# A weight load of 128 partitions cut into 32 and 96 at the head of a streamed bilinear kernel

## The chip, the cores and the metric

The kernel runs on one core of a Trainium2 chip. The metric is the device time of one execution in microseconds, the median of several runs. The profile's span is a little shorter than that time: it runs from the first to the last instruction that the profiler records.

## What is computed

```python
def setup_inputs():
    batch, dim_i, dim_j, dim_k = 32, 256, 256, 128
    # x [32, 256], y [32, 256], weight [128, 256, 256], all float32

def reference(x, y, weight):
    return np.einsum('bi,bj,kij->bk', x, y, weight).astype(np.float32)
```

For each of the 128 values of k there is a matrix of 256 x 256, and the output is x W_k y for every row of the batch. The weights are 128 x 256 x 256 x 4 B = 33.6 MB, and each is used once per row of the batch, so the kernel is in the main a stream of the weights from memory.

## The kernel before

The 128 matrices are handled as 32 groups of four. A group lies on chip as 128 partitions: partition p belongs to matrix p mod 4 of the four (`KK = 4`) and to row block p // 4 of the matrix (`IP = 32` blocks of `IC = 8` rows). Each partition has 8 x 256 = 2,048 elements of the group, one contiguous run of 8,192 bytes in memory. This view of the weights is made here:

```python
    def rows_of(groups):
        step = G // len(groups)
        v = weight.rearrange("(u s) (ip ic) j -> s ip u (ic j)", s=step, ic=IC)
        return v[groups[0]]
```

For one group it has the shape 32 x 4 x 2,048: the slowest dimension in memory is the row block, of size 32.

Thirty of the groups are loaded by GpSimd's software queue in eleven transfers (`LOADS`), which cast float32 to bfloat16 on the way into `w_sb`. They are large at first and small at the end, so that little work is left when the last one lands. Two groups, `FIRST = (0, 16)`, go another way: they are loaded as float32 into a buffer `w_f` by the hardware queues of SyncE and ScalarE, and ScalarE casts them into `w_sb`.

```python
LOADS = (
    ((8, 24), 0, 8),
    ((4, 12, 20, 28), 0, 8),
    (tuple(range(2, 32, 4)), 0, 8),
    (tuple(range(1, 32, 4)), 0, 8),
    # ... smaller and smaller
    ((31,), 7, 8),
)
FIRST = (0, 16)

    sw = [
        nc.gpsimd.dma_start(
            out=w_of(groups)[:, :, lo * J:hi * J],
            in_=rows_of(groups)[:, :, lo * J:hi * J],
        ).then_inc(s, 16).ins
        for (groups, lo, hi), s in zip(LOADS, s_w)
    ]
    # the load of y is put behind the second of them

    hw = [
        nc.scalar.dma_start(out=x_sb, in_=x).then_inc(s_x, 16).ins,
    ]
    for n, (g, queue) in enumerate(zip(FIRST, (nc.sync, nc.scalar))):
        hw.append(
            queue.dma_start(
                out=w_f[:, n:n + 1, :], in_=rows_of((g,)),
            ).then_inc(s_f[n], 16).ins
        )
```

All these issues are moved to the very head of the program, ahead of its opening instructions. The cast of the two first groups on ScalarE:

```python
    for n, g in enumerate(FIRST):
        for h in range(2):
            lo, hi = h * IC * J // 2, (h + 1) * IC * J // 2
            c = act.copy(out=w_sb[:, place_of[g], lo:hi], in_=w_f[:, n, lo:hi])
            if h == 0:
                c._wait_ge(s_f[n], 16)
            c.then_inc(s_act, 1)
```

VectorE meanwhile builds `xblk`, x arranged as stationary matrices, and `y4`, y repeated over the partitions. TensorE then works through units of 16, 8, 4, 2, 1 and 1 groups (`UNITS`), each matmul waiting for the load that brings its weights; VectorE multiplies the sums by `y4` and adds them up into `acc`, which SyncE stores.

```python
    pe.wait_ge(s_act, 2 * len(FIRST))
    pe.wait_ge(s_dve, t_x)
    # for each unit: 8 steps of matmuls, each waiting for its load
            c = product(
                ps[:, bank + h, :n, :],
                xblk[:, ic, :, :].rearrange("p b kk -> p (b kk)"),
                w_sb[:, p0 + o:p0 + o + n, ic * J:(ic + 1) * J],
                # ...
            )
            if need:
                c._wait_ge(need[-1], 16)
    # then on VectorE: tmp = ps * y4, acc = sum of tmp over j

    sp.dma_start(out=out_v, in_=acc)._wait_ge(s_dve, n_dve).then_inc(s_out, 16)
```

Of the kernel before, what the change touches and what calls it, by code (L numbers as in the profile page):

```python
# [29 lines left out]
)  # L30

FIRST = (0, 16)
BANKS = 8


@with_exitstack
def kernel(
# [7 lines left out]
    nc = tc.nc  # L45
# [10 lines left out]
    KK = P // B  # L56
# [9 lines left out]
    def sbuf(name, shape, dtype):  # L66
        return nc.alloc_sbuf_tensor(name, shape, dtype).ap()

    def rows_of(groups):


        step = G // len(groups)
        assert all(g == groups[0] + n * step for n, g in enumerate(groups))
        v = weight.rearrange("(u s) (ip ic) j -> s ip u (ic j)", s=step, ic=IC)
        return v[groups[0]]

    def w_of(groups):
        at = [place_of[g] for g in groups]
        step = at[1] - at[0] if len(at) > 1 else 1
        assert all(a == at[0] + n * step for n, a in enumerate(at))  # L80
        return w_sb[:, at[0]:at[-1] + 1:step, :]

    w_sb = sbuf("w_sb", [P, G, IC * J], bf16)
    w_f = sbuf("w_f", [P, len(FIRST), IC * J], f32)
    x_sb = sbuf("x_sb", [B, I], f32)
# [10 lines left out]
    acc = sbuf("acc", [P, G], f32)  # L96
    ps = nc.alloc_psum_tensor("ps", [P, BANKS, 2, J], f32).ap()

# [4 lines left out]
        for s, (groups, lo, hi) in zip(s_w, LOADS) for g in groups for ic in range(lo, hi)  # L103
    }
    s_f = [nc.alloc_semaphore(f"f{g}") for g in FIRST]
    s_x = nc.alloc_semaphore("x")
# [14 lines left out]
            out=w_of(groups)[:, :, lo * J:hi * J],  # L121
            in_=rows_of(groups)[:, :, lo * J:hi * J],
# [6 lines left out]
    hw = [  # L129
        nc.scalar.dma_start(out=x_sb, in_=x).then_inc(s_x, 16).ins,  # L130
    ]
    for n, (g, queue) in enumerate(zip(FIRST, (nc.sync, nc.scalar))):
        hw.append(
            queue.dma_start(
                out=w_f[:, n:n + 1, :], in_=rows_of((g,)),
            ).then_inc(s_f[n], 16).ins
        )
    for ins in [*hw, *sw]:
        tc.no_tile_sem_insts.add(ins.name)

# [8 lines left out]
    for blk in blocks:  # L149
# [20 lines left out]
        out=ident, in_=ident, compare_op=mybir.AluOpType.not_equal, fill=1.0,  # L170
# [3 lines left out]

    for n, g in enumerate(FIRST):
        for h in range(2):
            lo, hi = h * IC * J // 2, (h + 1) * IC * J // 2
            c = act.copy(out=w_sb[:, place_of[g], lo:hi], in_=w_f[:, n, lo:hi])  # L178
            if h == 0:
                c._wait_ge(s_f[n], 16)  # L180
            c.then_inc(s_act, 1)


# [2 lines left out]
    def done(ins):  # L186
# [6 lines left out]
        out=x_rep,  # L193
        in_=x_sb.rearrange("b (ip ic) -> b ic ip", ic=IC).unsqueeze(3)
        .to_broadcast([B, IC, IP, KK]),
    )._wait_ge(s_x, 16))
    for q in range(Q):
        c = v.transpose(  # L198
            out=xt[q * 32:(q + 1) * 32, :, :],
            in_=x_rep[:, :, q * IP // Q:(q + 1) * IP // Q, :],  # L200
        )
# [4 lines left out]
        out=mask, in_=ident.rearrange("p (ip kk) -> p kk ip", kk=KK), axis=AX, op=add,  # L206
    )._wait_ge(s_pool, 2))

    for kk in range(KK):
        c = v.tensor_scalar(  # L210
            out=xblk[:, :, :, kk], in0=xt, scalar1=mask[:, kk:kk + 1],
            scalar2=None, op0=mult,
        )
# [6 lines left out]
        out=yt, in_=y_sb.rearrange("b (jb j) -> b jb j", j=32),  # L220
    )._wait_ge(s_y, 16))
    t = done(v.tensor_copy(  # L222
        out=y_rep, in_=yt.unsqueeze(3).to_broadcast([B, J // 32, B, KK]),
    )._wait_ge(s_dve, t))
    BQ = B // Q
    for q in range(Q):
        c = v.transpose(  # L227
            out=y4[q * 32:(q + 1) * 32, :].rearrange("p (jb j) -> p jb j", j=32),
            in_=y_rep[:, :, q * BQ:(q + 1) * BQ, :],
        )  # L230
# [5 lines left out]
    def product(out, lhsT, rhs, first, last, load):  # L236
        return pe.add_instruction(mybir.InstMatmult(  # L237
            name=nc.get_next_instruction_name(), engine=mybir.EngineType.PE,
            ins=[pe.lower_ap(rhs), pe.lower_ap(lhsT)], outs=[pe.lower_ap(out)],
            start_tensor_calc=first, stop_tensor_calc=last,  # L240
            tile_size=(P, P), tile_position=(0, 0), ldweights=load,
        ))

    pe.wait_ge(s_act, 2 * len(FIRST))
    pe.wait_ge(s_dve, t_x)
    at_dve = t_x
    n_pe = 0
    freed = [0] * BANKS
    landed = set()
    p0 = bank = 0  # L250
    held = None
    for u, unit in enumerate(UNITS):

        n_g = len(unit)
        n_b = (n_g + 1) // 2
        if bank + n_b > BANKS:
            bank = 0
# [8 lines left out]
        for n_step, (ic, h) in enumerate(steps):  # L266
            n = n_g // n_b
# [7 lines left out]
            for s in need[:-1]:  # L275
                pe.wait_ge(s, 16)
# [4 lines that stand above are left out]
                first=(ic == order[0]), last=(ic == order[-1]), load=(held != ic),  # L281
            )
# [10 lines left out]
        if n_g > 1:  # L293
            t = done(v.tensor_tensor(  # L294
                out=prod, in0=sums, in1=y4.unsqueeze(1).to_broadcast([P, n_g, J]), op=mult,
# [3 lines left out]
                out=acc[:, unit[0]:unit[-1] + 1:unit[1] - unit[0]], in_=prod, axis=AX, op=add,  # L299
            )._wait_ge(s_dve, t))  # L300
        else:
            done(v.tensor_tensor_reduce(  # L302
                out=prod[:, 0, :], in0=sums[:, 0, :], in1=y4, scale=1.0, scalar=0.0,
# [44 lines left out]
```

## Time and profile before

| what | value |
|---|---|
| time, median of 3 runs | 84.98 us (84.9 to 85.03) |
| span of the profiled execution | 83.4 us |
| TensorE busy | 32.5 us (39%) |
| VectorE busy | 25.2 us (30%) |
| ScalarE busy | 5.2 us (6%) |
| GpSimd busy | 8.8 us (11%) |
| read from memory | 33.62 MB, 403 GB/s over the span |
| first float32 group (SyncE's queue), issue to landing | 4.9 us |
| second float32 group (ScalarE's queue), issue to landing | 8.3 us |

The profile is of one execution. Its page has the busy time of each engine, the span in 40 equal slices (a digit is the busy share in tenths; DMA is the mean over the core's 16 DMA engines), the DMA queues with packets, megabytes and the time of their packets, the chain of work that ended last, groups of instructions by line, and the DMA issues. Other views of the same trace list who waited for whom (total, times, longest), the chain piece by piece (start, length, what), instructions in order of time (start, length, what) and the busy time of each engine in chosen stages. PE is TensorE, PEld its weight load, DVE VectorE, ACT ScalarE, POOL GpSimd, SP SyncE; L134 is line 134 of the kernel. An engine's name with a q behind it (SPq) is the sequencer that issues.

### The profile page before, as it was taken

How to read it: one execution, taken by the hardware profiler on the slowest of the kernel's cores; microseconds unless marked ns; L12 is line 12 of the kernel's file. 1: busy time of each engine (PE TensorE's matmuls, PEld its weight loads, DVE VectorE, ACT ScalarE, POOL GpSimd, SP SyncE). 2: the span in 40 equal slices, each digit the busy share in tenths (PEclk: the TensorE clock that was granted, in tenths of full speed). 3: DMA queues.
4: the chain of work that ended last, by engine and by line, in shares of the span. 5: the costliest groups of instructions: out<-in, count | busy, mean ns of one | idle time of the engine just before them, and what ended most of it. 6: DMA issues, size and time to landing. Idle time of an engine off the chain costs nothing.

```text
span 83.4 us, 257 instructions
## 1 busy us (share of the span) xinstructions
PE 32.5 (39%) x136; PEld 4.3 (5%) x43; DVE 25.2 (30%) x28; ACT 5.2 (6%) x5; POOL 8.8 (11%) x18
## 2 busy tenths in 40 slices
PE   0000000000000000000099999996029999884780
PEld 0000000000000000000000000000000110112330
DVE  0009450000292000000000000003999800999932
ACT  0019930000000000000000000000000000000000
POOL 5999600000000000000000000000000000000000
PEclk9999999999999999999999999999995799999998
DMA  4999999999999999999999999999999999999980
GB/s 122 393 370 293 214 214 212 216 218 212 218 218 216 212 216 216 212 218 214 212 214 218 210 220 214 214 214 216 212 214 218 212 214 216 212 216 214 197 118 8
DMA packets 4912, 17.91 MB, mean 215 GB/s; under 512 B 384, under 2 KB 800, under 8 KB 4656
## 3 DMA queue, kind: packets, MB, share of 16 engines
q0 software_dynamic: 4432, 15.76, 94.4%
q1 hardware_dynamic: 288, 1.07, 3.5%
q10 hardware_dynamic: 192, 1.08, 3.3%
HBM read 33.62 MB, written 0.02 MB: 403 GB/s over the span
## 4 chain that ended last, share of the span: by engine, by line
DMA 46%; PE 39%; DVE 6%; POOL 3%; another core or an unknown queue 3%; issue 2%; POOLq 0%
DMA w_sb<-in_weight_dram 46%; PE ps L237 39%; DVE tmp L294 5%; POOL w_sb L120 2%; POOL y_sb L127 1%; DVE tmp L302 1%; POOL const-float32-0.0 L332 0%; POOLq L332 0%; POOL const-uint8-127 L332 0%; POOL const-float32-1.0 L332 0%; DVE acc L302 0%
## 5 line engine op out<-in xcount | busy, mean ns | idle before, releaser
L237 PE MATMUL ps<-w_sb,xblk 128*128 128x512 bf16 (+1 forms) x136 | 32.5, 396 | 48.9 <-DMA w_sb<-in_weight_dram 44.2
L294 DVE TENSOR_TENSOR tmp<-ps,y 128x4096 f32<-128x4096 f32 (+3 forms) x4 | 8.6, 2156 | 36.7 <-PE ps L237 36.6
L298 DVE TENSOR_REDUCE acc<-tmp 128x16 f32<-128x4096 f32 (+3 forms) x4 | 8.6, 2154 | 0.1
L237 PEld LDWEIGHTS ps<-w_sb,xblk 128*128 128x128 bf16 x43 | 4.3, 101 | 76.9 <-DMA w_sb<-in_weight_dram 42.7
L120 POOL DMA_DIRECT2D w_sb<-in_weight_dram x11 | 7.6, 707 | 0.6 <-issue 0.6
L178 ACT CAST w_sb<-w_f 128x1024 bf16<-128x1024 f32 x4 | 3.9, 1040 | 0.0
L219 DVE STREAM_TRANSPOSE yt<-y_sb 32x256 f32<-32x256 f32 x1 | 0.4, 433 | 10.9 <-DMA y_sb<-in_y_dram 10.9
L192 DVE COPY x_rep<-x_sb 32x1024 f32<-32x1024 f32 x1 | 0.8, 790 | 6.1 <-PEq L332 6.1
L227 DVE STREAM_TRANSPOSE y<-y_rep 32x256 f32<-32x256 f32 x4 | 1.7, 435 | 0.1
L198 DVE STREAM_TRANSPOSE xt<-x_rep 32x256 f32<-32x256 f32 x4 | 1.7, 435 | 0.1
L178 ACT ACT_TABLE_LOAD x1 | 1.3, 1283 | 6.0 <-PEq L332 6.0
L210 DVE TENSOR_SCALAR xblk<-xt,mask 128x256 bf16<-128x256 f32 x4 | 1.4, 499 | 0.0
L302 DVE CUSTOM_DVE_ANT_0 tmp<-ps,y 128x256 f32<-128x256 f32 x2 | 0.8, 424 | 1.6 <-PE ps L237 1.6
L222 DVE COPY y_rep<-yt 32x1024 f32<-32x1024 f32 x1 | 0.7, 682 | 0.0
L205 DVE TENSOR_REDUCE mask<-ident 128x4 f32<-128x128 f32 x1 | 0.4, 382 | 1.0 <-POOL ident L169 1.0
L127 POOL DMA_DIRECT2D y_sb<-in_y_dram x1 | 0.5, 534 | 0.0
L168 POOL MEMSET ident<- 128x128 f32 x1 | 0.3, 302 | 0.0
L169 POOL TENSOR_SCALAR_AFFINE_SELECT ident<-ident 128x128 f32<-128x128 f32 x1 | 0.3, 287 | 0.1
L302 DVE DVE_READ_ACCUMULATOR2_ANT acc<- 128x1 f32 x2 | 0.2, 84 | 0.0
L332 POOL MEMSET const-float32-0.0<- 128x1 f32 x1 | 0.1, 98 | 0.2 <-issue 0.2
L332 POOL MEMSET const-bfloat16-1.0<- 128x1 bf16 x1 | 0.1, 101 | 0.0
L332 POOL MEMSET const-uint8-127<- 128x1 uint8 x1 | 0.1, 101 | 0.0
(1 smaller groups left out, 0.1 us busy)
## 6 DMA issues: line engine op xcount, KB each, us to landing
w_sb<-in_weight_dram POOLq DMA_DIRECT2D x2, 4096.0 KB, 48.0
w_sb<-in_weight_dram POOLq DMA_DIRECT2D x2, 2048.0 KB, 43.3
w_sb<-in_weight_dram POOLq DMA_DIRECT2D x2, 1024.0 KB, 40.9
w_f<-in_weight_dram SPq DMA_DIRECT2D x1, 1024.0 KB, 4.9
w_f<-in_weight_dram ACTq DMA_DIRECT2D x1, 1024.0 KB, 8.3
w_sb<-in_weight_dram POOLq DMA_DIRECT2D x1, 512.0 KB, 72.1
w_sb<-in_weight_dram POOLq DMA_DIRECT2D x1, 256.0 KB, 72.7
w_sb<-in_weight_dram POOLq DMA_DIRECT2D x1, 128.0 KB, 72.9
```

Source lines behind the costliest of these rows:

```text
L120: nc.gpsimd.dma_start(out=w_of(groups)[:, :, lo * J:hi * J], in_=rows_of(groups)[:, :, lo * J:hi * J],).then_inc(s, 16).ins
L127: sw.insert(2, nc.gpsimd.dma_start(out=y_sb, in_=y).then_inc(s_y, 16).ins)
L178: c = act.copy(out=w_sb[:, place_of[g], lo:hi], in_=w_f[:, n, lo:hi])
L192: t = done(v.tensor_copy(out=x_rep, in_=x_sb.rearrange("b (ip ic) -> b ic ip", ic=IC).unsqueeze(3) .to_broadcast([B, IC, IP, KK]),)._wait_ ...
L198: c = v.transpose(out=xt[q * 32:(q + 1) * 32, :, :], in_=x_rep[:, :, q * IP // Q:(q + 1) * IP // Q, :],)
L210: c = v.tensor_scalar(out=xblk[:, :, :, kk], in0=xt, scalar1=mask[:, kk:kk + 1], scalar2=None, op0=mult,)
L222: t = done(v.tensor_copy(out=y_rep, in_=yt.unsqueeze(3).to_broadcast([B, J // 32, B, KK]),)._wait_ge(s_dve, t))
L227: c = v.transpose(out=y4[q * 32:(q + 1) * 32, :].rearrange("p (jb j) -> p jb j", j=32), in_=y_rep[:, :, q * BQ:(q + 1) * BQ, :],)
L237: return pe.add_instruction(mybir.InstMatmult(name=nc.get_next_instruction_name(), engine=mybir.EngineType.PE, ins=[pe.lower_ap(rhs), pe.l ...
L294: t = done(v.tensor_tensor(out=prod, in0=sums, in1=y4.unsqueeze(1).to_broadcast([P, n_g, J]), op=mult,)._wait_ge(s_pe, n_pe))
L298: done(v.tensor_reduce(out=acc[:, unit[0]:unit[-1] + 1:unit[1] - unit[0]], in_=prod, axis=AX, op=add,)._wait_ge(s_dve, t))
L302: done(v.tensor_tensor_reduce(out=prod[:, 0, :], in0=sums[:, 0, :], in1=y4, scale=1.0, scalar=0.0, op0=mult, op1=add, accum_out=acc[:, uni ...
```

## The change

The first float32 group, on SyncE's queue, is loaded in two transfers in place of one: partitions 0 to 31, and then partitions 32 to 127. On the memory side that is row blocks 0 to 7 and 8 to 31. Both add 16 to the same semaphore, and the cast waits for 32. The second float32 group keeps its one transfer. The small first piece is meant to be under way before the rest of the group has been issued.

```diff
 FIRST = (0, 16)
+
+FIRST_PARTS = (((0, 32), (32, 128)), ((0, 128),))
 BANKS = 8
@@
-    for n, (g, queue) in enumerate(zip(FIRST, (nc.sync, nc.scalar))):
-        hw.append(
-            queue.dma_start(
-                out=w_f[:, n:n + 1, :], in_=rows_of((g,)),
-            ).then_inc(s_f[n], 16).ins
-        )
+    for n, pieces in enumerate(FIRST_PARTS):
+        for lo, hi in pieces:
+            hw.append(
+                (nc.sync, nc.scalar)[n].dma_start(
+                    out=w_f[lo:hi, n:n + 1, :],
+                    in_=rows_of(FIRST[n:n + 1])[lo // KK:hi // KK],
+                ).then_inc(s_f[n], 16).ins
+            )
@@
             if h == 0:
-                c._wait_ge(s_f[n], 16)
+                c._wait_ge(s_f[n], 16 * len(FIRST_PARTS[n]))
             c.then_inc(s_act, 1)
```

## The prediction

> **What bounds the kernel now.** I read the page's utilisation in slices first, to see which unit never rests, then the queue table, then the waits and the chain, and last the stage table and the issues.
>
> The slices and the queue table of the page:
>
> ```profile
> PE   0000000000000000000099999996029999884780
> ...
> DMA  4999999999999999999999999999999999999980
> GB/s 122 393 370 293 214 214 212 216 218 212 218 218 216 212 216 216 212 218 214 212 214 218 210 220 214 214 214 216 212 214 218 212 214 216 212 216 214 197 118 8
> ...
> q0 software_dynamic: 4432, 15.76, 94.4%
> q1 hardware_dynamic: 288, 1.07, 3.5%
> q10 hardware_dynamic: 192, 1.08, 3.3%
> ```
>
> The reader is to see that the 16 DMA engines are at nine tenths or more from the second slice to the last but two, while TensorE does nothing for half of the span. GB/s counts bytes as they land: about 390 while float32 lands as float32, 215 while the software queue q0 casts float32 to bfloat16 on the way, so 430 GB/s as they are read. In q1 stand the first float32 group (the transfer that is changed) and the output; in q10 x and the second float32 group.
>
> The waits, then pieces of the chain that ended last:
>
> ```profile
> PE ps L237 <- DMA w_sb<-in_weight_dram: 44.2, 5, 41.9
> ...
> DVE yt L219 <- DMA y_sb<-in_y_dram: 10.9, 1, 10.9
> ```
>
> ```profile
> 3.18 38.65 DMA w_sb<-in_weight_dram
> ...
> 41.87 15.66 PE ps L237 x64
> ...
> 80.42 0.66 PE ps L237 x3
> 81.09 0.03 issue
> 81.12 0.30 PE ps L237
> 81.42 0.02 issue
> 81.44 0.42 DVE tmp L302
> ```
>
> TensorE's first matmul waits 41.9 us for loads, and its last one starts at 81.12, right behind the last load (the trace has that load's sixteen completion updates between 80.59 and 81.07 us). So the end is: last weight byte landed, plus a tail of 83.4 - 81.07 = 2.3 us. The middle of the chain goes over PE and DVE, but there too loads arrive one after another without a pause in the DMA row, and what TensorE is behind in the middle it has made up when the small last loads come. What moves the last landing moves the end by the same amount; nothing else that this change touches does.
>
> The stage table (length, busy of PE, PEld, DVE, ACT, POOL, then clock, DMA share, GB/s) and the two issues at the start:
>
> ```profile
> 2.00:5.00 3.00, 0.00 (x0) 0.00 (x0) 0.00 (x0) 0.00 (x0) 3.00 (x5) 1.00 1.01 401
> ...
> 20.00:40.00 20.00, 0.00 (x0) 0.00 (x0) 2.85 (x6) 0.00 (x0) 0.00 (x0) 1.00 1.06 215
> ```
>
> ```profile
> 0.00 0.63 SPq L134 DMA_DIRECT2D w_f<-in_weight_dram  x1
> 0.12 0.42 ACTq L130 DMA_DIRECT2D x_sb<-in_x_dram  x1
> ```
>
> From the first table comes the price of one row of 8,192 bytes on one DMA engine. In the stage 20 to 40: 2 x 215 / 16 = 26.9 GB/s read per engine, so 8,192 B take 0.305 us. In the float32 stage 2 to 5: 401 / 16 = 25.1 GB/s, 0.327 us; most single packet records there last 0.309 us. I take 0.31 us.
>
> [...] No transfer of the kernel before shows a number under 16: [...] the trace agrees with 16 (q1 has 288 packets: 128 rows and 16 completions for w_f, 128 and 16 for the output). [...] q1's eight rows per engine all go ahead of q10's (first q10 row at 4.19 us), and only then do q10 and q0 mix.
>
> **The change part by part.**
>
> *Removed:* one transfer of 128 rows, 8,192 B each. On 16 engines that is 8 rows per engine.
>
> *Added, first piece:* memory side 8 x 4 rows, chip side 32 partitions. [...] engines 0 to 7 get 4 rows each. *Second piece:* memory side 24 x 4, chip side 96; [...] engines 0 to 11 get 8 rows each. [...] Together: engines 0 to 7 have 12 rows, engines 8 to 11 have 8, engines 12 to 15 none, in place of 8 each. All other transfers still give each engine a sixteenth. Every load waits for its slowest engine, and the kernel is bound by DMA to the end, so engines 0 to 7 carry their 4 extra rows to the last load: 4 x 0.31 = +1.24 us. Engines 12 to 15 end 8 x 0.31 = 2.5 us early, which nobody uses.
>
> *Moved, the start:* the first packet of w_f starts at 1.42 us (packet records), 1.42 after its issue began. The 32-row load of x, issued at 0.12, starts at 1.16, 1.04 after. Their issues last 0.63 and 0.42 us in the timeline above. A 32-row piece of w_f should then start like x, 0.2 to 0.38 us earlier: I take -0.3 us, for just the engines that have the extra rows. The second piece, issued behind it, starts near 0.42 + 1.42 = 1.84 us; the four rows of the first piece keep engines 0 to 7 busy to beyond 2.2 us, so there is no hole.
>
> *Moved, which engine is last:* the sixteen completions of a load lie 0.48 us apart throughout (the first q0 load 11.97 to 12.45, the last 80.59 to 81.07). If the engines are late in the order of their numbers, because they are started in that order, engines 0 to 7 are some 0.28 us ahead of the last one (its eighth completion is at 12.17) and the shift shrinks by so much; the records don't name the engine. I take half, -0.15 us.
>
> *Beside other work:* one more issue on SyncE (0.6 us, which has nothing else to do before the output), a wait for 32 in place of 16, and a first group that lands later than 4.9 us. ScalarE's first cast starts at 7.33 us, behind its table load, and its four casts last 3.9 us; even 2.5 us more would end them at 14 us, and TensorE begins at 41.9. Cost 0.
>
> Sum: 1.24 - 0.3 - 0.15 = +0.8 us, from 84.98 to 85.8. For the second rival below I take 0.1 off: 85.7.
>
> **The rivals.**
>
> 1. *All 16 engines still carry both pieces* [...]. Then no engine has more rows, and the earlier start alone stays: -0.2 to -0.4, 84.6 to 84.8 us. It is what the change seems to be for. For it: the trace shows no transfer on fewer engines. [...] About one in five.
>
> 2. *The engines share one limit* (memory as a whole), and engines 0 to 7 run faster while 12 to 15 have nothing. Then the sum of bytes counts, and the time stays at 84.7 to 85.1 us. For it: all sixteen move at one pace, 0.48 us apart from first to last. Against it: the same 0.309 us packets stand at very different moments, and a few undisturbed 8,192 B packets before the span, with hardly another one in flight, last 0.307 to 0.333 us, so a row has its own price. One in ten.
>
> 3. *A hole at the start*: if descriptors of the second piece come behind those of x and of the second float32 group, engines may rest between the pieces. This would add 0.2 to 0.6 us, to about 86.3 us. One in twelve.
>
> **Range and chances.** The main case spans +0.55 to +1.25 us (both reductions in full, or none), 85.5 to 86.2; rivals 1 and 2 reach down to 84.6, rival 3 up to 86.3. So 85.7, with 84.6 to 86.3 as the range. Slower by over 2% means over 86.68, +1.7 us, which needs more than the extra rows and a hole together: 0.04. Faster by over 2% means under 83.28, and a start 1.7 us earlier isn't there to be had, since the first byte moves at 1.2 us: 0.01. Within 2%: 0.95.
>
> **What would show it.** The packets of q1: 32 + 8 + 96 + 12 + 144 = 292 if the pieces run on 8 and 12 engines, 32 + 16 + 96 + 16 + 144 = 304 on 16 each. The completions of every later load should lie about 3 us apart (12 rows against none) in place of 0.48, and the DMA row should sag in the last two slices, below the 9 and 8 of before. First w_f packet: near 1.05 us. Last landing: 81.07 + 0.8 = 81.9 us, with the tail of 2.3 us unchanged. The prediction is wrong if q1 has 304 packets, if completions stay within half a microsecond, or if an uneven load leaves the last landing where it was.

## The result, and the profile after

The changed kernel takes 88.88 us (median of 6 runs, 88.45 to 89.13), the kernel before beside it 84.91 us (84.69 to 85.03). The ratio is 1.0467, with a 95% interval of 1.0438 to 1.0497: slower by 4.0 us. The prediction was 85.7 us, with a range up to 86.3, and it gave 0.04 to a loss of more than 2%.

The slices and the queues of the changed kernel, in the same rows as before (share of DMA engines busy, GB/s landed; then packets, megabytes, and the time of the packets as a share of 16 engines' span):

```profile
DMA  1999999999999999999999999999999999999860
GB/s 45 341 349 197 204 180 206 212 212 216 218 218 216 214 221 212 212 216 216 216 214 218 212 214 216 214 219 214 212 216 214 214 219 216 212 208 195 155 92 8
...
q0 software_dynamic: 4432, 15.76, 90.6%
q1 hardware_dynamic: 292, 1.07, 5.6%
q10 hardware_dynamic: 192, 1.08, 3.6%
```

Two things stand here. First, q1 has 292 packets: 256 rows, 128 of the group and 128 of the output, and 36 completion records of 4 B, 8 behind the small piece (3.20 to 3.26 us), 12 behind the larger (12.94 to 13.68) and 16 behind the output. Taken as one record an engine, the pieces run on 8 and on 12 engines, as predicted; the 32 rows of the small piece also start in four rounds of eight (1.77 to 1.89 us, 2.22 to 2.30, 2.56 to 2.63, 2.88 to 2.94). The records do not name the engine: engines 0 to 7 are here a name for the eight of the small piece, 0 to 11 for the twelve of the larger, and that the eight are among the twelve is assumed. Second, q1 carries the same 1.07 MB and takes far longer over it: 5.6% of 16 x 87.4 us is 78 us of engine time, where it was 3.5% of 16 x 83.4 us, 47 us. The 31 us more are 2.6 us for each of twelve engines, if they are spread evenly. By the packet records some 25 of them lie in the rows of 8,192 B, the rest in the 4 B completion records behind the second piece. The DMA row is full as before from the second slice on, although slices 4 to 6 land 197, 204 and 180 GB/s, where it was 293, 214 and 214: here a busy engine wasn't one that gets on.

The waits, then the chain piece by piece, after the change:

```profile
PE ps L241 <- DMA w_sb<-in_weight_dram: 47.9, 4, 45.9
...
DVE yt L223 <- DMA y_sb<-in_y_dram: 14.9, 1, 14.9
```

```profile
3.18 42.65 DMA w_sb<-in_weight_dram
...
85.12 0.30 PE ps L241
```

TensorE's first wait has grown from 41.9 to 45.9 us, and y, queued behind the second software load, is waited for 14.9 us in place of 10.9. So all 4.0 us are lost before y lands, at 26.4 us, and nothing is lost later: the last load lands at 85.07 in place of 81.07, and the tail behind it is 2.3 us as before. The loss shows in the stage from 9 us to 14.6, first after, then before:

```profile
9.00:14.60 5.60, 0.00 (x0) 0.00 (x0) 1.74 (x5) 0.01 (x1) 0.66 (x3) 1.00 1.13 192
```

```profile
9.00:14.60 5.60, 0.00 (x0) 0.00 (x0) 1.75 (x5) 2.22 (x3) 0.66 (x3) 1.00 1.06 213
```

192 is less than 213, although part of the 192 is float32, which lands more bytes in the same time (in the kernel before 401 GB/s from 2 to 5 us, when no cast row moved, and 215 from 20 to 40, when all were cast). In the packet records a row of 8,192 B of the second piece takes 0.55 to 0.78 us in this time; a float32 row of q10 beside the software queue took 0.322 us before. It is not so from the first row on: the 20 rows of the piece that start between 5.1 and 6.3 us take 0.31 to 0.39 us, the 76 later ones 0.49 to 0.79. All 96 together take 58.1 us, 0.61 each. The start differs too: the issues now last 1.70 us for two,

```profile
0.00 1.70 SPq L137 DMA_DIRECT2D w_f<-in_weight_dram  x2
```

about 0.83 us each in place of one of 0.63; the first row starts at 1.77 us (1.42 before), and the engines that have no row of the small piece start only at 2.70 us, with q10. This last number varies: in a kernel below with the same pieces (rows that lie next to each other) it is 2.07 us, at nearly the same time, 88.97 us.

### The profile page after: what moved, and what is told of

Read it like the earlier page. It is cut to its first block, busy times and chain, and to the rows that moved or that the text cites. A ratio compares the mean times of both kernels' runs of the same rounds, so it can differ in the third digit from the quotient of the medians.

```text
span 87.4 us, 258 instructions
## 1 busy us (share of the span) xinstructions
PE 32.7 (37%) x136; PEld 4.3 (5%) x43; DVE 25.0 (29%) x28; ACT 5.2 (6%) x5; POOL 8.8 (10%) x18
## 3 DMA queue, kind: packets, MB, share of 16 engines
q1 hardware_dynamic: 292, 1.07, 5.6%
## 4 chain that ended last, share of the span: by engine, by line
DMA 49%; PE 37%; DVE 6%; POOL 3%; another core or an unknown queue 2%; issue 1%; POOLq 0%
DMA w_sb<-in_weight_dram 49%; PE ps L241 37%; DVE tmp L298 5%; POOL w_sb L122 2%; POOL y_sb L129 1%; DVE tmp L306 0%; POOL const-float32-0.0 L336 0%; POOLq L336 0%; POOL const-float32-1.0 L336 0%; POOL const-uint8-127 L336 0%; DVE acc L306 0%
## 5 line engine op out<-in xcount | busy, mean ns | idle before, releaser
L223 DVE STREAM_TRANSPOSE yt<-y_sb 32x256 f32<-32x256 f32 x1 | 0.4, 432 | 14.9 <-DMA y_sb<-in_y_dram 14.9
```

## The experiments

The theory after the result, P: a row's price depends on where it lands. Some sets of partitions, written at one time, would make a row take up to twice as long, about 0.6 us in place of 0.31. Which sets these are was the author's estimate ahead of each run; no trace so far had shown it. The rivals: R, the rows on the fullest engine count and nothing else; Q, a transfer on fewer than 16 engines is slow as such; D, the reads collide in memory. All times stand beside 84.8 us of the kernel before on the same chip. In the queue views the packets include the 4 B completion records; rows are counted here from the megabytes, at 8,192 B each.

### 64 and 64 partitions

```diff
-FIRST_PARTS = (((0, 32), (32, 128)), ((0, 128),))
+FIRST_PARTS = (((0, 64), (64, 128)), ((0, 128),))
```

> The first group in two pieces of 64 partitions: [...] both run on 16 engines, 4 rows an engine, and no engine has more rows than before (304 packets in q1). Theory P (where a piece lands decides[...]): [...] rows of each piece take about 0.6 us in place of 0.31 where nothing else runs, 4 x 0.3 for each piece: +1.2 to +2.4 us, 86.1 to 87.3. Rival R (only the number of rows on the fullest engine counts): 84.6 to 85.2, rows at 0.31 us.

Measured: 86.02 us, ratio 1.0140 (1.0120 to 1.0161), +1.2. q1 has 304 packets: 256 rows and 48 completion records, 16 of them behind the output, so 16 for each piece, read as 16 engines with four rows each, even loads. The queue view from 2.5 to 4.5 us (packets, MB, share of 16 engines):

```profile
q1 hardware_dynamic: 37, 0.17, 40.9%
```

0.17 MB are 21 rows, and 40.9% of 32 us of engine time is 13.1 us: 0.62 us a row, the records showing 0.606 again and again, nearly twice the 0.309 us of most rows in the kernel before. R falls, since by these counts no engine has a row more. The time is just under the expected span: the rows of the second piece mix with others and take 0.41 us on average.

### More rows in a buffer that nothing reads

The kernel before with one more transfer behind the first, on the same queue. The group's partitions 0 to 31, 32 to 127, or all of them, are loaded a second time (the buffer `w_d`, its semaphore and a wait for it at the end are left out here):

```diff
+    hw.append(
+        nc.sync.dma_start(
+            out=w_d[0:32, :], in_=rows_of((0,))[0 // KK:32 // KK],   # or 32:128, or 0:128
+        ).then_inc(s_d, 16).ins
+    )
```

> The kernel before, with one more transfer behind the first on the same queue: partitions 0 to 31 of the same group once more, into a buffer that nothing reads. It adds 4 rows to each of engines 0 to 7 and nothing else. Both theories: +4 x 0.31 = +1.24 us or a little less, 85.8 to 86.2[...]. If few engines as such were slow, as in a rival Q (a hardware-queue row on a transfer of fewer than 16 engines takes 0.75 us beside the software queue), +2.5 to +3, 87.5 to 88.

> The kernel before, with one more transfer behind the first on the same queue: partitions 32 to 127 of the same group once more, into a buffer that nothing reads[...]. Theory P: 8 rows at some 0.65 to 0.75 us, +5 to +6 us, about 90.3, rows of q1 visibly longer from the moment that q0 runs. Rival R (rows count alone): 8 x 0.31 = +2.5 us, 87.4. In both engines 12 to 15 land their part of each load early.

> The kernel before, with the whole first group loaded once more on the same queue, into a buffer that nothing reads: 16 engines, 8 rows each[...]. Both theories: 8 x 0.31 = +2.5 us, 87.4. Beside the run with 96 extra partitions this is the test: under P the larger transfer costs about half of the smaller one, under R they cost the same.

Measured: 85.82 us for 32 partitions (ratio 1.0110, 1.0084 to 1.0137), 89.69 for 96 (1.0574, 1.0550 to 1.0598), 87.56 for 128 (1.0309, 1.0276 to 1.0341). So +1.0, +4.9 and +2.7 us: 96 rows cost 1.8 times what 128 rows cost. That is a little less than the 5 to 6 us that P had for the 96, and nearly twice the 2.5 that R had. The queues of the runs with 96 and with 128:

```profile
q1 hardware_dynamic: 396, 1.85, 7.3%
```

```profile
q1 hardware_dynamic: 432, 2.11, 6.5%
```

1.85 MB took 7.3% of 16 x 88.6, 103 us of engine time; 2.11 MB took 6.5% of 16 x 86.5, 90 us. The packets over the 288 of the kernel before are 108 and 144: 96 rows with 12 completion records, and 128 with 16. The run with 32 shows what four rows more on engines 0 to 7 cost with partitions 0 to 31 as their destination: 1.0 us, close to the prediction's 1.24 less 0.15. It is no slower for being on 8 engines, which speaks against Q.

### The same reads, two destinations

48 rows read twice more, expected on 12 engines; the only difference between the two kernels is the destination.

```diff
+    for m in range(2):
+        hw.append(
+            nc.sync.dma_start(
+                out=w_d[32:80, m, :], in_=rows_of((0,))[8:20],   # the other kernel: w_d[0:48, m, :]
+            ).then_inc(s_d, 16).ins
+        )
```

> The kernel before, with 48 rows of the same group loaded twice more behind the first transfer, on the same queue, into partitions 32 to 79 of a buffer that nothing reads. 12 row blocks in memory and 48 partitions: 12 engines, 4 rows an engine and transfer, 8 more rows for each of engines 0 to 11. [...] Theory P: 8 x 0.31 less the 0.25 us that engines 0 to 7 are ahead, +2.2 to +2.5 us, 87.0 to 87.4, rows of q1 at 0.32 us beside q0. Rival Q (a transfer on 12 engines is slow as such): +4.5 to +5 as with the 96 extra partitions, 89.4 to 89.8.

> The same, with the same 48 rows read, into partitions 0 to 47. Nothing differs from the run into partitions 32 to 79 but where the rows land[...]. Theory P: rows of those eight engines up to 0.6 us, 8 x 0.3 on top, +4 to +5 us, 88.8 to 89.8. Rivals (rows count, engines, or where the rows are read): the same time as into partitions 32 to 79.

Measured: 87.42 us into partitions 32 to 79 (1.0304, 1.0286 to 1.0322), 88.30 into 0 to 47 (1.0412, 1.0385 to 1.0439). The queue view from 10 to 12.5 us, first 32 to 79, then 0 to 47:

```profile
q1 hardware_dynamic: 47, 0.36, 35.6%
```

```profile
q1 hardware_dynamic: 38, 0.29, 37.5%
```

0.36 MB are 44 rows in 14.2 us, 0.32 us each; 0.29 MB are 35 rows in 15.0 us, 0.43 each, and up to 0.50 in the records. The first run is as expected and ends Q: its +2.6 us are the 8 x 0.32 of eight rows more on each of twelve engines, so twelve are not slow as such. The second is slower by 0.9 us through its destination alone, as P has it, but I expected about 2, and 88.30 lies below the expected span. I had counted eight rows at twice the price throughout; the rows rose by a third, from 0.32 to 0.43 us. Why 0 to 47 is the dearer destination, and by no more than this, is not shown: that it would be was the author's estimate.

### Rows that lie next to each other in memory

```diff
+    near = weight.rearrange("k (a b) j -> (k a) (b j)", b=IC).rearrange(
+        "(m s) f -> m s f", s=8)[:24, :4]
...
-                    in_=rows_of(FIRST[n:n + 1])[lo // KK:hi // KK],
+                    in_=(
+                        near if (n, lo) == (0, 32)
+                        else rows_of(FIRST[n:n + 1])[lo // KK:hi // KK]
+                    ),
```

> The changed kernel, with the second piece of 96 partitions read from rows that lie next to each other in memory (24 blocks of four neighbouring rows) in place of four rows 8 MB apart; the first group of weights is then not the right one, all sizes, engines and destinations stay. Theory P: nothing changes, 88.5 to 89.1, rows of q1 still at 0.6 to 0.75 us. Rival D (the reads of the twelve engines collide in memory): rows at 0.32 us, 86.0 to 86.6.

Measured: 88.97 us (1.0507, 1.0469 to 1.0545); the kernel computes the first group from other rows of the weights, but moves as many. The queue view from 9 to 13 us of this kernel, then of the changed kernel:

```profile
q1 hardware_dynamic: 48, 0.39, 52.1%
```

```profile
q1 hardware_dynamic: 48, 0.39, 51.2%
```

48 rows in 33 us, 0.69 us each in both. Between these two layouts, where the rows are read from does not matter: D falls.

### All 128 partitions, cut by columns

```diff
-FIRST_PARTS = (((0, 32), (32, 128)), ((0, 128),))
+FIRST_PARTS = (((0, 512), (512, 2048)), ((0, 2048),))
...
-                    out=w_f[lo:hi, n:n + 1, :],
-                    in_=rows_of(FIRST[n:n + 1])[lo // KK:hi // KK],
+                    out=w_f[:, n:n + 1, lo:hi],
+                    in_=rows_of(FIRST[n:n + 1])[:, :, lo:hi],
```

> The first group in two transfers of all 128 partitions, the first 512 of the 2,048 columns and then the other 1,536: a small first portion, as the change meant[...]. P and rows count: no engine has more, so within 0.3 us of before, 84.6 to 85.2. If a smaller first portion gets the engines going earlier (as the prediction had it), 84.4 to 84.7; the issue has as many rows as before, so I expect the first packet at 1.4 us as before.

Measured: 87.33 us (1.0299, 1.0276 to 1.0323), +2.5. No theory of mine had this. The queue view from 1.5 to 3.5 us, and for comparison the kernel before from 2 to 4:

```profile
q1 hardware_dynamic: 104, 0.20, 50.0%
```

```profile
q1 hardware_dynamic: 101, 0.83, 101.7%
```

Both queues start about 100 packets in 2 us. With rows of 8,192 B that is just what 16 engines use up; with rows of 2,048 B it is a quarter of the bytes, and the engines stand half idle. It looks as if rows were handed to the engines at some 50 a us whatever their size. But in the kernel before the full engines may have set that pace. And of x in that kernel, 32 rows of 1,024 B on the other hardware queue, all rows but one began within 0.3 us of each other, so there is no such limit for every transfer. The cause stays open. It is another loss than that of the change: its later rows, at 0.247 us for 6,144 B, are not held up (three quarters of the 0.322 us of a row of 8,192 B are 0.242).

### Four pieces of 32

```diff
+FIRST_PARTS = (((0, 32), (32, 64), (64, 96), (96, 128)), ((0, 128),))
```

> The first group in four pieces of 32 partitions: 8 engines each, 16 rows for each of engines 0 to 7, none for the others. That is the most uneven of all (8 rows more than before on the fullest engine, where the changed kernel has 4). Theory P [...]: [...] rows near 0.31 us, and +8 x 0.31, less 0.25 that these engines are ahead, plus 0.4 for the later start: 87.4 to 88.2, no slower than the changed kernel at 88.9. Rival R (the fullest engine's rows, each at what the changed kernel paid for its four, 1 us a row): +8 us, about 93.

Measured: 87.21 us (1.0297, 1.0268 to 1.0326), 0.2 below the expected span. The most uneven of all loads, if each piece takes the same eight engines: 16 rows on each of engines 0 to 7 and none on the others. It costs 2.44 us over the kernel before beside it, close to 8 x 0.31 = 2.5 for eight rows more, where the changed kernel costs 3.97. The queue view from 8 to 13 us:

```profile
q1 hardware_dynamic: 72, 0.47, 23.4%
```

0.47 MB are 57 rows in 18.7 us of engine time: 0.33 us each, where the changed kernel paid 0.69.

### The larger piece first, and other partitions

```diff
+FIRST_PARTS = (((32, 128), (0, 32)), ((0, 128),))   # one kernel
+FIRST_PARTS = (((0, 96), (96, 128)), ((0, 128),))   # another
```

> The two pieces in the other order, partitions 32 to 127 first and then 0 to 31: the same rows on the same engines, but the 96 rows now run before the software queue has begun. Theory P: part of these rows already takes about 0.6 us at 2 to 5 us, when only the hardware queues run[...]; less is lost than in the changed kernel[...]: 86.8 to 88. Rival Q0 (only the mixing with the software queue makes them slow): rows at 0.31 us until 5 us and 86.0 to 86.5.

> Partitions 0 to 95 in the first piece and 96 to 127 in the second: the same sizes and engines, other destinations. Theory P: again rows of 0.6 us before q0 runs[...]: 86.8 to 88, near the run with partitions 32 to 127 first. If only the piece's size counted and not its place, the two would be the same within 0.3 us.

Measured: 89.13 us (1.0514, 1.0488 to 1.0540) and 88.60 us (1.0444, 1.0419 to 1.0469), both above what I expected. The queue view of the first from 4 to 7 us, before the software queue has moved a row:

```profile
DMA packets 69, 0.50 MB, mean 167 GB/s; under 512 B 8, under 2 KB 8, under 8 KB 8
...
q1 hardware_dynamic: 44, 0.29, 62.5%
q10 hardware_dynamic: 25, 0.20, 44.5%
```

167 GB/s with all engines busy is what six of them move at the 26.9 GB/s that each read from 20 to 40 us in the kernel before. In the records the rows climb to 0.91 and 0.94 us at 6 us, three times 0.305, and those of q10 with them. So the software queue, whose first row moves at 8.56 us in this run (5.48 in the kernel before), isn't needed for the loss. The place counts as well as the size: with partitions 0 to 95 first the rows reach 0.64 us by 7 us, and not 0.94. Which engine writes which partitions of a 96-row piece is not in the records, and why one place is dearer than the other stays open.

### The small piece ahead of the whole group

As the run with 32 extra partitions, with the extra transfer issued first:

```diff
     hw = [
         nc.scalar.dma_start(out=x_sb, in_=x).then_inc(s_x, 16).ins,
     ]
+    hw.append(
+        nc.sync.dma_start(
+            out=w_d[0:32, :], in_=rows_of((0,))[0 // KK:32 // KK],
+        ).then_inc(s_d, 16).ins
+    )
     for n, (g, queue) in enumerate(zip(FIRST, (nc.sync, nc.scalar))):
         # ... the whole first group, then the second, as before
```

> As the run with 32 extra partitions (85.8), but with the extra transfer ahead of the whole first group on SyncE's queue: it takes the start of the changed kernel alone, a small piece on 8 engines ahead[...]. In the changed kernel the first row began at 1.77 us in place of 1.42 and the engines without rows of the small piece at 2.70. If that start costs what it seems (0.35 us on engines 0 to 7, 1.28 on the others): the others then become the last, +1.1 to +1.5, engines 0 to 7 +1.3: 86.0 to 86.4. If the prediction's early start were right: engines 0 to 7 0.3 us earlier than with the extra piece behind, 85.5.

Measured: 86.21 us (1.0180, 1.0148 to 1.0212), as expected. This is the changed kernel's start in kind (the first row at 1.67 us, the engines without a row of the small piece at 2.21), and the same twelve rows on engines 0 to 7 and eight on engines 8 to 11, but with eight more on engines 12 to 15, and its pieces are of 32 and of 128 partitions, the sizes that as extra transfers cost only 1.0 and 2.7 us. It takes 86.21 - 84.77 = 1.44 us more than before; the changed kernel takes 88.88 - 84.91 = 3.97.

## Why the prediction was wrong

1. *What bounds the kernel.* Right. The end moved by as much as the last landing (4.0 us), the tail stayed 2.3 us, and ScalarE's casts, now from 14.6 to 18.5 us, cost nothing.

2. *8 and 12 engines.* An estimate that no trace of the kernel before showed. Right: 292 packets, with 8 and 12 completion records. The completions of the last load lie from 80.33 to 85.07 us, four early and twelve late. That is more than the 3 us predicted, and engines 8 to 11 are among the late ones, though on the assumption above they have no row more than before. Their late start, 1.28 us, explains only a part of that; counting rows is not enough. The early four were to end 2.5 us ahead of where they did before and end some 0.3 us ahead (80.33 to 80.73, where all sixteen had 80.59 to 81.07): their late start took 1.28 us of that, and the rest was not traced.

3. *Four more rows, +1.24 us, less 0.15.* Right: the extra 32 partitions alone cost 1.0 us. In that run's first software load eight completions come at 12.07 to 12.39 us and eight at 13.17 to 13.30, so the loaded eight had been about 0.3 us ahead of the slowest.

4. *The earlier start, -0.3 us.* Wrong in sign. The small piece takes longer to issue (0.83 us in place of 0.63), its first row starts at 1.77 us and not at 1.05, and the engines without a row of it wait until 2.70. I had taken x's load, on 16 engines, as the model. Put ahead in place of behind, the small transfer costs 1.44 - 0.99 = +0.45 us (give or take some 0.35, by the two intervals). This is the hole of rival 3, in another place: not between the pieces, but on the engines that the first piece leaves out.

5. *0.31 us for every row.* This step failed, and made most of the miss. The price was read from transfers of 128 partitions, and I used it for a piece of 96. In the changed kernel a row of that piece takes 0.61 us on average over its 96 rows, and 0.69 from 9 to 13 us. For eight rows an engine that is 8 x (0.61 - 0.31) = 2.4 us. The times say the same: the changed kernel takes 3.97 - 1.44 = 2.5 us more than the run with a like start and the same rows on engines 0 to 11. With the terms of steps 3 and 4 the packet records give 0.99 + 0.45 + 2.4 = 3.8 us, of 3.97 measured.

What is shown: the destination alone can make rows dear (two kernels that differ in nothing else, 0.9 us apart, with rows at 0.32 and 0.43 us); rows come at 0.606 us in a piece of 64 partitions, and at up to 0.94 in one of 96; neither the reads, nor the number of engines, nor the mixing with the software queue is needed. What makes a destination dear is not shown. For the 96 rows of the change P is an inference from smaller transfers: which engine writes where is not known, and why the first 20 rows were cheap (0.31 to 0.39 us) stays open. Rivals 1 and 2 are out: the loads are uneven, and the four engines that end early help nobody, as the shift stays 4.0 us to the end. One ground against rival 2 was read too kindly, though: of the packets of 8,192 B before the span there are six, and two of them last 0.381 and 0.549 us, not 0.307 to 0.333.

## What to carry to other kernels

Ask of a cut transfer how many DMA engines each piece gets and where it lands, before counting bytes: here pieces of 32 and 96 partitions left 8 and 12 completion records in place of 16, and a price of 0.31 us a row, read from full 128-partition transfers, became 0.61 in the piece of 96. No version here, by partitions or by columns, beat the one whole transfer; of the cuts by partitions, two pieces of 64 cost the least (+1.2 us), then four of 32 (+2.4), and those with a piece of 96 the most (+3.8 to +4.4). And compare a queue's share of engine time with its bytes: a DMA row at nine tenths hid here a queue that took 1.7 times as long over the same bytes (78 us for 47).

## What was not expected of the hardware

A 96-row transfer costs more than a 128-row one (+4.9 against +2.7 us). Rows of 2,048 B at the head of the stream moved at 102 GB/s, with about 50 begun per us. And the order of the hardware queues at the start: the second float32 group's first row went at 4.19 us in the kernel before, behind all but one of the 128 rows of the first, but at 2.70 us in the changed kernel, between the two pieces.
